# A transformer block on one core: Strassen's scheme on 2x2 blocks for the gates, the convolution inputs and the up projection

## The chip, the core and the metric

The kernel runs on one core of a Trainium2 chip. The metric is the device time of one execution in microseconds (us). A core has five engines that run side by side, each through its own instructions in order: PE (TensorE, the matrix products; its weight loads are listed as PEld), DVE (VectorE), ACT (ScalarE), POOL (GpSimd) and SP (SyncE, which issues nearly all DMAs here). PE writes its products into PSUM, eight banks of 128 partitions x 512 fp32 values; everything else lives in SBUF or, through DMAs, in DRAM.

## The reference

The input is x, 1024 rows of 1024 channels. All numbers are fp32.

```python
h = rms_norm(x, norm1_g)
q, k, v, bg, cg, xc = split(h @ w_in)                 # six times 1024 columns
y_attn = chunked_relpos_attention(q, k, v, ...)       # 16 heads, chunks of 64, 8 chunks back
y_conv = bg * (conv_b + depthwise_causal_conv3(cg * xc, conv_w))
g_attn, g_conv = split(sigmoid(h @ w_gate + b_gate))  # w_gate: 1024 x 2048
merged = g_attn * (y_attn @ w_attn_proj) + g_conv * (y_conv @ w_conv_proj)
x = x + merged @ w_out
h2 = rms_norm(x, norm2_g)
u = square(relu(h2 @ w_up))                           # w_up: 1024 x 4096
x = x + u @ w_down                                    # w_down: 4096 x 1024
```

## The kernel before, in words

Activations lie transposed: channels on the 128 partitions, the 1024 sequence positions along the free dimension, in two halves of 512 (`HC`). A product makes, for one output tile of 128 channels and one half, a sum in one PSUM bank over K in k-tiles of 128. To keep fp32 accuracy, each operand is held as a pair: `split` (L81) makes a high part with an ACT copy and a low part, source minus high part, with a DVE subtraction. A k-tile then costs three matmuls of 128x128 by 128x512 (high by high, low by high, high by low), pinned in the order of the code on PE by `pin` (L69).

The stages, in order of time:
- Attention, pair of heads by pair of heads, with the first `NG = 5` of 16 gate tiles woven into the last pair (L528 to L562). The operand `hT` (normalised rows without the row factor, which `rb` brings in later) stands in SBUF as two tiles of 32 KB a partition.
- The gate tiles 5 to 15 (L568), each 2 halves x 8 k-tiles x 3 = 48 matmuls through `t_stages` (L127); the results, times `rb`, go to DRAM (`gD`).
- The three convolution inputs for each of 8 tiles (L582 to L610), 48 matmuls a product, and the convolution on DVE; its result is split into `yc`, which stays in SBUF.
- The projections `cp` (L628), `ap` (L637) and `out` (L652), 384 matmuls each. Their operands `yc`, `aoT`, `mT`, `h2T` are written into SBUF in split form as their producers come out of PSUM.
- Up and down, woven (L723 to L727): 256 of the 4096 hidden channels are made (`up`, 96 matmuls), and while the next 256 are made, these are used (`down`, 96 matmuls over K = 256) and added to 16 accumulators in SBUF (L719). The mean square of the second norm (two fp32 matmuls by ones, a reciprocal on DVE, L672 to L677) sits in the first up group.

Weights come by DMA into a `raw` tile, are split into a `w` tile of a rotating pool, and are used. Each engine's order is made by a planner that runs when the kernel is built: it takes instructions whose inputs and buffers are ready in the order in which the code has them, so a load or a split moves ahead as far as its buffer allows; matmuls stay in the code's order. A pool opened in the space of closed pools waits for the last reader of every tile in the closed pools that it overlaps (unless it asks for less, which neither kernel does).

Of the kernel before, what the change touches and what calls it, by code (L numbers as in the profile page):

```python
# [40 lines left out]
def block_kernel(ctx, tc, x, xt, wqkv, wcnv, wgate, wcp, wap, wout, wup, wdown,  # L41
# [9 lines left out]
    apool = ctx.enter_context(tc.tile_pool(name="apool", bufs=2))  # L51
    dram = ctx.enter_context(tc.tile_pool(name="dram", bufs=1, space=DRAM))
    psmm = ctx.enter_context(tc.tile_pool(name="psmm", bufs=2, space=PSUM))
# [21 lines left out]
    def matmul(ps, lhsT, rhs, start, stop):  # L75
        pin(nc.tensor.matmul(ps, lhsT, rhs, start=start, stop=stop))  # L76
# [33 lines left out]
    def load_t(src, name):  # L110
        return [load_w(src[u], [4, P], f"{name}_{u}") for u in range(2)]
# [8 lines left out]
    banks = [(psmm, "mm")] * 2  # L120
# [6 lines left out]
    def t_stages(src, mov, evac, name, order=None):  # L127
# [6 lines left out]
        def mm(c, kt):  # L134
            def go():
                if kt == 0:
                    st[c] = bank(f"ps_{name}_{c}")
                w = st["w"][kt // 4]
                for n, (i, j) in enumerate(((0, 0), (1, 0), (0, 1))):
                    matmul(st[c][:], w[:, i, kt % 4, :], mov[c][:, j, kt, :],  # L140
                           kt == 0 and n == 0, kt == ND - 1 and n == 2)
# [5 lines left out]
    def t_layout(*a):  # L147
        load, halves = t_stages(*a)
        load()
        for h in halves:  # L150
            for f in h:
                f()

    def new_act(name):
        return [apool.tile([P, 2, ND, HC], F32R, name=f"{name}{c}", tag="act") for c in range(2)]


    hT = new_act("hT")
# [11 lines left out]
    aoD = [[dram.tile([P, HC], F32, name=f"aoD{p}_{c}") for c in range(2)]  # L170
           for p in range(NH // 2)]
    gD = [dram.tile([P, S], F32, name=f"gD{t}") for t in range(16)]
    mcD = [dram.tile([P, S], F32, name=f"mcD{t}") for t in range(ND)]

# [41 lines left out]
    def qkv_stages(p):  # L216
# [39 lines left out]
        def evac(st, ps):  # L256
            hf, s4 = st // 4, st % 4
            qk = ps[:, 0:256].rearrange("p (a b) -> p a b", a=4)
            sq = a1.tile([P, 4, DH], F32, name=f"sq{p}_{st}", tag="sq")
# [78 lines left out]
    def unit_stages(p, c, m, h):  # L338
# [61 lines left out]
        def pv(g):  # L400
            def go():
# [11 lines left out]
                if g == len(groups) - 1:  # L413
# [6 lines left out]
                    if m % 2 and h:  # L420
                        nc.sync.dma_start(aoD[p][m // 2][:], c.ao[:])
# [97 lines left out]
    def gate_stages(t):  # L519
        def ev(c, ps):  # L520
            g = a1.tile([P, HC], F32, name=f"gp{t}_{c}", tag="sq")
            nc.vector.tensor_tensor(g[:], ps[:], rb[:, c * HC:(c + 1) * HC], op=ALU.mult)
            nc.sync.dma_start(gD[t][:, c * HC:(c + 1) * HC], g[:])
        load, halves = t_stages(wgate[t], hT, ev, f"g{t}")
# [40 lines left out]
    wpool = ctx.enter_context(tc.tile_pool(name="wpool", bufs=2, side="right"))  # L565
    psx = ctx.enter_context(tc.tile_pool(name="psx", bufs=6, space=PSUM))
    banks = [(psx, "x")] * 3 + [(psmm, "mm")] + [(psx, "x")] * 3 + [(psmm, "mm")]
# [215 lines left out]
```

## Time and profile before

| | us |
|---|---|
| median of 3 runs (1910.05 to 1911.23) | 1910.75 |
| the profiled execution | 1911.13 |
| its span, from the first to the last instruction | 1909.3 |
| PE busy with matmuls (9268 of them) | 1882.7 |
| DVE busy | 1058.8 |
| ACT busy | 560.7 |
| POOL busy | 164.0 |

The span leaves 1.8 us of the profiled execution outside. A busy time counts how long an engine had an instruction in work; an engine that is busy all the time is not thereby at its peak. The granted clock of TensorE is a share of 2.4 GHz; its other level is 1.2 GHz (0.5).

### The profile page before, as it was taken

The numbers are of one execution on the slowest core, as the hardware profiler recorded it, in microseconds if no ns is written. First come the engines' busy times: TensorE is split into PE (matmuls) and PEld (weight loads), VectorE is DVE, ScalarE is ACT, GpSimd is POOL, SyncE is SP. The second block draws the span as 40 slices with busy tenths as digits, with TensorE's granted clock in tenths as the row PEclk, the third lists the DMA queues.
The fourth block names the chain that finished last, engine by engine and source line by source line (L and its number), as shares of the span: only waits on it lengthen the run. The fifth ranks groups of instructions, "written<-read, shape, count | busy, mean of one in ns | idle before, by whom it ended". The sixth has DMA issues, their size and how long they took to land.

```text
span 1909.3 us, 24631 instructions
## 1 busy us (share of the span) xinstructions
PE 1882.7 (99%) x9268; PEld 1614.8 (85%) x9268; DVE 1058.8 (55%) x1966; ACT 560.7 (29%) x1117; POOL 164.0 (9%) x467
## 2 busy tenths in 40 slices
PE   6899999999999999999999999999999999999999
PEld 6899999999888888888888888888888888888887
DVE  6677877787642234435433445655555555555555
ACT  5455555555431111111232333211111111111110
POOL 5433233233000000000000000000000000000000
PEclk9999999999999999999999999999999999999999
DMA  6443443443322211111364451111111111111112
GB/s 245 111 109 92 104 110 92 111 110 88 111 86 96 94 56 50 50 45 51 109 215 143 144 156 54 36 53 50 50 45 49 52 45 50 50 45 44 50 51 93
DMA packets 91031, 162.08 MB, mean 85 GB/s; under 512 B 10912, under 2 KB 19104, under 8 KB 90912
## 3 DMA queue, kind: packets, MB, share of 16 engines
q1 hardware_dynamic: 90768, 160.48, 28.7%
q8 instruction: 73, 1.20, 0.3%
q14 instruction: 46, 0.38, 0.1%
q10 hardware_dynamic: 144, 0.03, 0.0%
HBM read 114.33 MB, written 20.97 MB: 71 GB/s over the span
## 4 chain that ended last, share of the span: by engine, by line
PE 95%; POOL 2%; DMA 1%; DVE 1%; ACT 1%; issue 0%; SPq 0%; DVEq 0%; POOLq 0%; ACTq 0%
PE ps_u L76 18%; PE pd L76 18%; PE psq L76 12%; PE ps_g L76 9%; PE ps_x L76 5%; PE ps_cp L76 5%; PE ps_o L76 5%; PE ps_ap L76 5%; PE ps_b L76 5%; PE ps_c L76 5%; PE av L76 3%; PE s L76 3%; PE tp L79 3%; POOL qw L115 0%; PE tq L79 0%
## 5 line engine op out<-in xcount | busy, mean ns | idle before, releaser
L76 PE MATMUL psq<-w_q,hT 128*128 128x384 f32 x1536 | 347.9, 352 | 11.2 <-ACT w_q L83 7.6
L76 PE MATMUL ps_u<-h2T,w_u 128*128 128x512 f32 x1536 | 355.2, 392 | 0.0
L76 PE MATMUL pd<-ut,w_d 128*128 128x512 f32 x1536 | 354.0, 391 | 0.0
L76 PEld LDWEIGHTS ps_u<-h2T,w_u 128*128 128x128 f32 x1536 | 288.5, 188 | 63.9 <-issue 1.0
L76 PEld LDWEIGHTS pd<-ut,w_d 128*128 128x128 f32 x1536 | 288.4, 188 | 63.1
L76 PEld LDWEIGHTS psq<-w_q,hT 128*128 128x128 f32 x1536 | 261.7, 193 | 15.2 <-ACT w_q L83 7.6
L719 DVE TENSOR_TENSOR acc<-pd,acc 128x512 f32<-128x512 f32 x256 | 176.5, 690 | 109.9 <-PE pd L76 107.7
L76 PE MATMUL ps_g<-hT,w_g 128*128 128x512 f32 x768 | 187.9, 395 | 0.0
L76 PEld LDWEIGHTS ps_g<-hT,w_g 128*128 128x128 f32 x768 | 140.6, 188 | 27.2
L689 DVE SCALAR_TENSOR_TENSOR rq<-ps_u,rb 128x512 f32<-128x512 f32 x64 | 44.2, 691 | 135.6 <-PE ps_u L76 135.5
L364 ACT ACTIVATE p<-p,sm 128x640 f32<-128x640 f32 (+4 forms) x128 | 89.7, 701 | 80.9 <-DVE sm L362 80.7
L83 ACT CAST ut<-rq 128x512 fp32r<-128x512 f32 x64 | 39.8, 622 | 216.1 <-DVE rq L691 216.1
L83 ACT CAST w_u<-r_u 128x512 fp32r<-128x512 f32 x64 | 39.9, 624 | 185.3 <-PE pd L76 107.7
L362 DVE CUSTOM_DVE_ANT_0 p<-s,b 128x640 f32<-128x640 f32 (+4 forms) x128 | 83.4, 652 | 12.8 <-PE s L76 9.6
L84 DVE TENSOR_TENSOR pt<-tp,pt 128x512 fp32r<-128x512 f32 (+1 forms) x144 | 84.2, 597 | 11.0 <-ACT pt L83 10.4
L76 PE MATMUL ps_x<-hT,w_x 128*128 128x512 f32 x384 | 89.2, 391 | 0.0
L76 PE MATMUL ps_c<-hT,w_c 128*128 128x512 f32 x384 | 89.2, 391 | 0.0
L76 PE MATMUL ps_b<-hT,w_b 128*128 128x512 f32 x384 | 89.2, 391 | 0.0
L76 PE MATMUL s<-k,q 128*128 128x384 f32 (+3 forms) x384 | 82.0, 322 | 6.4 <-DVE sm L362 6.2
L76 PEld LDWEIGHTS av<-pt,vt 128*128 128x128 f32 x576 | 85.5, 188 | 3.1 <-DVE pt L84 1.2
L83 ACT CAST w_d<-r_d 128x512 fp32r<-128x512 f32 x64 | 39.9, 623 | 164.2 <-PE pd L76 142.9
L76 PE MATMUL ps_cp<-yc,w_cp 128*128 128x512 f32 x384 | 88.1, 391 | 0.0
(116 smaller groups left out, 2232.0 us busy)
## 6 DMA issues: line engine op xcount, KB each, us to landing
q<-qh SPq DMA_DIRECT2D x128, 128.0 KB, 2.3
r_u<-in_wup_dram SPq DMA_DIRECT2D x64, 256.0 KB, 2.6
r_d<-in_wdown_dram SPq DMA_DIRECT2D x64, 256.0 KB, 2.7
r_q<-in_wqkv_dram SPq DMA_DIRECT2D x32, 384.0 KB, 3.5
k<-kh SPq DMA_DIRECT2D x64, 128.0 KB, 2.3
r_g<-in_wgate_dram SPq DMA_DIRECT2D x32, 256.0 KB, 2.7
gD<-gp SPq DMA_DIRECT2D x32, 256.0 KB, 2.0
gl<-gD SPq DMA_DIRECT2D x32, 256.0 KB, 2.9
```

Of the source, the lines that this page charges most:

```text
L76: pin(nc.tensor.matmul(ps, lhsT, rhs, start=start, stop=stop))
L79: pin(nc.tensor.transpose(o, i, ident[:]))
L83: return (nc.scalar.copy(hi, src), nc.vector.tensor_tensor(lo, src, hi.bitcast(F32), op=ALU.subtract))
L84: nc.vector.tensor_tensor(lo, src, hi.bitcast(F32), op=ALU.subtract))
L362: nc.vector.tensor_tensor_reduce(pw, sc[:, k0:k1], biast[p, h][:, 5 * P - w:], -1.0, 3e38, ALU.add, ALU.min, sm[:, 0:1])
L364: nc.scalar.activation(pw, pw, AF.Exp, bias=sm[:, 0:1], scale=-1.0, accum_out=sm[:, 1:2])
L689: nc.vector.scalar_tensor_tensor(q[:], ps[:], 0.0, rb2[:, cc], op0=ALU.max, op1=ALU.mult)
L719: nc.vector.tensor_tensor(a[:], ps[:], a[:], op=ALU.add)
```

## The change

Two neighbouring output tiles (256 channels), both halves of the sequence and two groups of four k-tiles are seen as 2x2 blocks: weights a11, a12, a21, a22 and operand blocks b11 to b22. Strassen's scheme (in Winograd's form) makes the four output blocks from seven block products in place of eight. Each block product sums over 4 k-tiles.

- It applies to 4 gate pairs (tiles 8 to 15), 12 convolution pairs (three inputs for each of 4 pairs of tiles) and 16 up pairs: 32 pairs. Gate tiles 5 to 7 stay plain and run ahead of them.
- The seven weight operands of a pair (`weights`): four loads, four POOL additions or subtractions, seven splits. `w` has 7 buffers, `raw` 5.
- The seven operand blocks (`slot`) are made once a stage, for four "slots" j of two k-tiles each: two source rows from DRAM (512 KB each), four POOL subtractions, seven splits. The `h` operand is made anew from x (`fetch_h`: load and a DVE multiply by gain and row factor); the `h2` operand goes through DRAM (`h2D`). Each slot tile takes 28 KB a partition; two lie on the left side of SBUF, two on the right.
- A narrow `product` runs the seven block products one after another, 12 matmuls each, in three banks: five of them go on adding into bank a, and between two of them ACT or DVE takes the sum so far out. A wide one (the first and the last of each of the two stages) goes through the slots outermost, with seven banks, and combines at the end.
- The other products are `plain`: operands are held per k-tile (8 KB), loaded from DRAM and split (`ktiles`), except for `mk`, which is written as before; the first three output tiles go through the k-tiles outermost with six banks, the last tile too.
- The convolution result (`yD`), the second norm's input (`x2D`, `h2D`) and the hidden activations (`uD`, 32 tiles) go through DRAM. Up runs whole, then down: four passes over K = 1024 each, 64 evictions in place of 256.
- h2 is scaled by `sp` = rb / (1 + rb) before up; the true factor `ms` comes in at the end, after the last pass. `sp` and `ms` take a reciprocal on DVE each.
- One pool of eight PSUM banks serves everything after attention.

The diff, cut to its core:

```diff
+    ps8 = ctx.enter_context(tc.tile_pool(name="ps8", bufs=8, space=PSUM))
+    banks = [(ps8, "x")]
+    jsr = ExitStack()
+    js = [jsr.enter_context(tc.tile_pool(name="jsr", bufs=2, side="right")), None]
...
+    bw = Work("bwa", 5, 2, 3)
+    PROD = {1: ("a11", 0), 2: ("a12", 1), 3: ("s4", 2), 4: ("a22", 6), 5: ("s1", 3),
+            6: ("s2", 4), 7: ("s3", 5)}
+    ORDER = (1, 2, 6, 7, 5, 4, 3)
+    def slot(j, name, fetch):
+        b = []
+        for r in range(2):
+            src = bw.stg(f"b{name}{j}_{r}")
+            fetch(src[:], 2 * j + r)
+            b.append([src[:, cols(c)] for c in range(2)])
+        o = js[j // 2].tile([P, 7, 2, HC], F32R, name=f"o{name}{j}", tag="js")
+        def put(i, x):
+            split(o[:, i, 0, :], o[:, i, 1, :], x)
+        def minus(i, x, y):
+            t = bw.tt(f"t{name}{j}_{i}")
+            nc.gpsimd.tensor_tensor(t[:], x, y, op=ALU.subtract)
+            put(i, t[:])
+            return t[:]
+        put(0, b[0][0])
+        t1 = minus(3, b[0][1], b[0][0])
+        put(1, b[1][0])
+        t2 = minus(4, b[1][1], t1)
+        put(2, b[1][1])
+        minus(5, b[1][1], b[0][1])
+        minus(6, b[1][0], t2)
+        return o
...
+    def weights(src, name):
+        a = {}
+        for n, k in enumerate(("a11", "a12", "a21", "a22")):
+            a[k] = fetch_w(src[n], [4, P], f"{name}_{k}")
+        w = {i: split_w(a[PROD[i][0]], f"{name}_{i}") for i in (1, 2)}
+        for k, x, y, op in (("s1", "a21", "a22", ALU.add), ("s2", "s1", "a11", ALU.subtract),
+                            ("s3", "a11", "a21", ALU.subtract), ("s4", "a12", "s2", ALU.subtract)):
+            if k in ("s1", "s2"):
+                a[k] = wk.tile([P, 4, P], F32, name=f"{name}_{k}", tag="ss", bufs=2)
+            else:
+                a[k] = a[{"s3": "a21", "s4": "a12"}[k]]
+            nc.gpsimd.tensor_tensor(a[k][:], a[x][:], a[y][:], op=op)
+        for i in ORDER[2:]:
+            w[i] = split_w(a[PROD[i][0]], f"{name}_{i}")
+        return w
...
+    def product(src, o, name, ev, wide=False, between=None):
+        w = weights(src, name)
+        if not wide:
+            a = bank(f"pa_{name}")
+            def whole(ps, i, start, stop):
+                for j in range(4):
+                    mms(ps, w, o, i, j, start and j == 0, stop and j == 3, True)
+            whole(a, 1, True, True)
...
+                s1 = snap(a, f"s1_{name}")
+            c = bank(f"pc_{name}")
+            whole(c, 2, True, True)
...
+                ev.put(0, 0, c, s1)
+            whole(a, 6, False, True)
...
+                u2 = snap(a, f"u2_{name}")
+            b = bank(f"pb_{name}")
+            whole(b, 7, True, True)
...
+                s7 = snap(b, f"s7_{name}")
+            whole(a, 5, False, True)
...
+                ev.put(1, 1, a, s7)
+            whole(b, 4, False, True)
...
+                ev.put(1, 0, b, u2)
+            whole(a, 3, False, True)
...
+                ev.put(0, 1, a, None)
+            return
...
+        for j in range(4):
+            for i in ORDER:
+                if j == 0:
+                    ps[i] = bank(f"p{i}_{name}")
+                mms(ps[i], w, o, i, j, j == 0, j == 3, False)
+        s1 = snap(ps[1], f"s1_{name}")
+        u2, u4 = etile(f"u2_{name}"), etile(f"u4_{name}")
+        nc.vector.tensor_tensor(u2[:], ps[6][:], s1[:], op=ALU.add)
...
+            ev.put(0, 0, ps[2], s1)
+        nc.vector.tensor_tensor(u4[:], ps[5][:], u2[:], op=ALU.add)
+        nc.vector.tensor_tensor(u2[:], ps[7][:], u2[:], op=ALU.add)
...
+            v = etile(f"u5_{name}")
+            nc.vector.tensor_tensor(v[:], ps[7][:], u4[:], op=ALU.add)
+        for (r, cc), p, e in (((0, 1), 3, u4), ((1, 0), 4, u2)):
...
+                ev.put(r, cc, ps[p], e)
...
+            ev.put(1, 1, None, v)
...
+        for n, (src, name, ev) in enumerate(jobs):
+            product(src, o, name, ev, n == 0 or free and n == len(jobs) - 1)
+    def fetch_h(d, kt):
+        nc.sync.dma_start(d.rearrange("p (s q) -> p s q", s=NT),
+                          xt[:, :, kt, :].rearrange("s p q -> p s q"))
+        nc.vector.scalar_tensor_tensor(d, d, sv[:, C_G1 + kt:C_G1 + kt + 1], rb[:],
+                                       op0=ALU.mult, op1=ALU.mult)
+    ho = [None] * 4
+    for j in range(2):
+        ho[j] = slot(j, "h", fetch_h)
+    for t in range(NG, 8):
         for f in gate_stages(t):
             f()
-    att.close()
+    aws.close()
+    hpool.close()
+    wk = ctx.enter_context(tc.tile_pool(name="wk", bufs=1))
+    wp = (wk, 7, 5)
+    nw = ctx.enter_context(tc.tile_pool(name="nw", bufs=1))
...
+    jsl = ExitStack()
+    js[1] = jsl.enter_context(tc.tile_pool(name="jsl", bufs=2))
+    for j in range(2, 4):
+        ho[j] = slot(j, "h", fetch_h)
...
+    jobs = [gate_job(4)] + sum([conv_jobs(i) for i in range(4)], [])
+    jobs += [gate_job(i) for i in range(5, 8)]
+    phase(jobs, ho, None, free=True)
+    cvs.close()
+    jsl.close()
+    bw.stack.close()
+    jsr.close()
+    def ktile(pool, name):
+        return pool.tile([P, 2, S], F32R, name=name, tag="kt", bufs=8)
+    def ktiles(pool, name, tiles, first=0):
+        out = []
+        for k in range(ND):
+            src = bw.stg(f"b{name}{k}")
+            nc.sync.dma_start(src[:], tiles[first + k][:])
+            o = ktile(pool, f"{name}{k}")
+            split(o[:, 0, :], o[:, 1, :], src[:])
+            out.append(o)
+        return out
+    def plain(src, o, name, ev, lead=3):
+        def group(ts, outer):
+            w = {t: [load_w(src[t // 2, 2 * (t % 2) + u], [4, P], f"{name}{t}_{u}")
+                     for u in range(2)] for t in ts}
...
+            if outer:
+                for kt in range(ND):
+                    for t in ts:
+                        for c in range(2):
+                            mm(t, c, kt)
...
+        group(list(range(lead)), True)
+        for t in range(lead, ND):
+            group([t], t == ND - 1)
+    kas, kbs = ExitStack(), ExitStack()
+    kta = kas.enter_context(tc.tile_pool(name="kta", bufs=1, side="right"))
+    ktb = kbs.enter_context(tc.tile_pool(name="ktb", bufs=1))
+    bw = Work("bwb", 4, 2, 0, side="left")
...
+    yk = ktiles(kta, "yk", yD)
+    ak = ktiles(ktb, "ak", aoD)
...
+    plain(wap, ak, "ap", ev_ap)
+    nc.vector.tensor_scalar(sp[:], rb[:], 1.0, None, op0=ALU.add)
+    nc.vector.reciprocal(sp[:], sp[:])
+    nc.vector.tensor_tensor(sp[:], sp[:], rb[:], op=ALU.mult)
+    bw.stack.close()
+    kbs.close()
+    jul = ExitStack()
+    js[0] = jul.enter_context(tc.tile_pool(name="jul", bufs=2))
+    bw = Work("bwc", 6, 2, 4, side="left")
...
+    def ev_out(t, c, ps):
...
+        nc.vector.tensor_tensor(a[:], ps[:], a[:], op=ALU.add)
+        nc.sync.dma_start(x2D[t][:, cols(c)], a[:])
+        h = bw.e(f"h{t}_{c}")
+        nc.vector.scalar_tensor_tensor(h[:], a[:], sv[:, C_G2 + t:C_G2 + t + 1],
+                                       sp[:, cols(c)], op0=ALU.mult, op1=ALU.mult)
+        nc.sync.dma_start(h2D[t][:, cols(c)], h[:])
...
+        if c == 1 and t in (1, 3):
+            h2o[t // 2] = slot(t // 2, "n", from_dram(h2D))
+    plain(wout, mk, "o", ev_out)
+    kas.close()
+    jur = ExitStack()
+    js[1] = jur.enter_context(tc.tile_pool(name="jur", bufs=2, side="right"))
+    for j in range(2, 4):
+        h2o[j] = slot(j, "n", from_dram(h2D))
...
+    phase([up_job(i) for i in range(16)], h2o, None, free=True)
+    ms = rb
+    for c in range(2):
+        ps = bank(f"ss2_{c}")
+        matmul(ps[:], ones[:], ssq[:, cols(c)], True, True)
+        m = ms[:, cols(c)]
+        nc.vector.tensor_scalar(m, ps[:], 1.0 / D, EPS, op0=ALU.mult, op1=ALU.add)
+        for _ in range(2):
+            nc.vector.tensor_tensor(m, m, sp[:, cols(c)], op=ALU.mult)
+        nc.vector.reciprocal(m, m)
+    ktd = ctx.enter_context(tc.tile_pool(name="ktd", bufs=1, side="right"))
+    bw = Work("bwd", 4, 2, 0)
...
+    def ktile(pool, name):
+        return pool.tile([P, 2, S], F32R, name=name, tag="kt", bufs=NKD)
+    NKD = 12
+    accp = ctx.enter_context(tc.tile_pool(name="accp", bufs=1))
+    acc = [accp.tile([P, S], F32, name=f"acc{t}") for t in range(ND)]
+    for k in range(4):
+        uk = ktiles(ktd, f"uk{k}_", uD, 8 * k)
+        def ev_d(t, c, ps):
+            a = acc[t][:, cols(c)]
+            if k == 0:
+                nc.scalar.copy(a, ps[:])
+            else:
+                nc.vector.tensor_tensor(a, ps[:], a, op=ALU.add)
+            if k == 3:
+                x2 = bw.e(f"xr{t}_{c}")
+                nc.sync.dma_start(x2[:], x2D[t][:, cols(c)])
+                nc.vector.tensor_tensor(a, a, ms[:, cols(c)], op=ALU.mult)
+                nc.vector.tensor_tensor(a, a, x2[:], op=ALU.add)
+                nc.sync.dma_start(out[t * P:(t + 1) * P, cols(c)], a)
+        plain(wdown[k], uk, f"d{k}_", ev_d)
+    bw.stack.close()
```

## Rows read from the trace of the kernel before

**Rows 1.** The page: busy time by engine; granted TensorE clock in 40 slices.

```profile
PE 1882.7 (99%) x9268; PEld 1614.8 (85%) x9268; DVE 1058.8 (55%) x1966; ACT 560.7 (29%) x1117; POOL 164.0 (9%) x467
...
PEclk9999999999999999999999999999999999999999
```

**Rows 2.** Critical chain, three stages: start us, length us, what.

```profile
673.28 10.99 PE ps_c L76 x48
...
1268.32 21.97 PE ps_u L76 x96
...
1861.60 43.97 PE pd L76 x192
```

**Rows 3.** Up and down: window, length, busy us by engine, clock, DMA.

```profile
1246.40:1861.60 615.20, 615.20 (x2689) 504.76 (x2688) 337.11 (x504) 104.72 (x168) 0.00 (x0) 1.00 0.17 48
```

**Rows 4.** Groups by form: line, engine, operation, xcount | busy us, mean ns.

```profile
L115 POOL TENSOR_TENSOR qw<-qw,nhalf 128x4 f32<-128x4 f32 x64 | 66.3, 1036 | 5.3
...
L84 DVE TENSOR_TENSOR w_u<-r_u,w_u 128x512 fp32r<-128x512 f32 x64 | 44.3, 693 | 13.0 <-ACT w_u L83 11.7
...
L691 DVE TENSOR_TENSOR rq<-ps_u,rq 128x512 f32<-128x512 f32 x64 | 44.0, 688 | 1.1
...
L83 ACT CAST w_u<-r_u 128x512 fp32r<-128x512 f32 x64 | 39.9, 624 | 185.3 <-PE pd L76 107.7 <-PE ps_u L76 64.8 <-PE ps_o L76 10.8
...
L268 POOL TENSOR_TENSOR qw<-qw 128x4 f32<-128x4 f32 x64 | 13.2, 207 | 5.3
...
L661 DVE SCALAR_TENSOR_TENSOR h2T<-acc,sv,h2T 128x512 fp32r<-128x512 f32 x16 | 12.0, 752 | 7.5 <-ACT h2T L660 6.4
...
L84 DVE TENSOR_TENSOR hT<-xt,hT 128x1024 fp32r<-128x1024 f32 x7 | 8.5, 1221 | 2.5 <-ACT hT L83 2.5
...
L203 ACT ACTIVATE xn<-xn 128x1024 f32<-128x1024 f32 x8 | 8.5, 1059 | 0.0
```

**Rows 5.** Line 677: min/median/max ns, first and last start us.

```profile
L677 DVE RECIPROCAL rb<-rb x2: 3353/3354/3354, 1205.0 to 1211.9; 128x512 f32<-128x512 f32 x2
```

**Rows 6.** DMA issues: count, KB each, median us to landing.

```profile
r_g<-in_wgate_dram SPq DMA_DIRECT2D x32, 256.0 KB, 2.7
...
gD<-gp SPq DMA_DIRECT2D x32, 256.0 KB, 2.0
...
acc<-in_xt_dram SPq DMA_DIRECT2D x16, 256.0 KB, 5.2
```

**Rows 7.** Timeline at attention's end: start us, length us, what.

```profile
551.06 9.29 PE L76 MATMUL ps_g<-hT,w_g 128*128 128x512 f32 x40
...
552.68 0.69 DVE L522 TENSOR_TENSOR gp<-ps_g,rb 128x512 f32<-128x512 f32 x1 [0.60 <-PE ps_g L76]
```

**Rows 8.** Timeline at the end of the convolution stage.

```profile
938.38 0.69 DVE L84 TENSOR_TENSOR yc<-y,yc 128x512 fp32r<-128x512 f32 x1
...
939.15 0.80 SPq L618 DMA_DIRECT2D a<-aoD  x2
```

**Rows 9.** Timeline of PE, idle time before it in brackets.

```profile
42.41 0.47 PE L79 MATMUL tq<-ident,qn 128*128 128x128 f32 x1 [4.08 <-DVE qn L279]
...
63.17 0.80 PE L76 MATMUL s<-k,q 128*128 128x256 f32 x2 [5.96 <-DVE sm L362]
```

**Rows 10.** Busy time after those idle stretches, columns as in Rows 3.

```profile
40.00:44.00 4.00, 1.59 (x7) 1.46 (x7) 2.07 (x4) 1.92 (x4) 2.78 (x6) 0.72 0.52 205
44.00:48.00 4.00, 3.38 (x11) 3.00 (x10) 2.41 (x3) 3.63 (x7) 3.59 (x6) 0.50 0.18 40
64.00:68.00 4.00, 4.00 (x14) 4.00 (x14) 1.90 (x8) 0.86 (x3) 0.00 (x0) 0.50 0.02 4
68.00:72.00 4.00, 4.00 (x25) 3.96 (x24) 2.03 (x8) 2.19 (x6) 1.79 (x5) 0.86 0.00 0
```

**Rows 11.** Timeline, last instruction before the final stores.

```profile
1905.59 0.69 DVE L719 TENSOR_TENSOR acc<-pd,acc 128x512 f32<-128x512 f32 x1 [0.69 <-PE pd L76]
```

More of the change, by code (lines that the diff above doesn't have):

```diff
@@ L73, in pin, with matmul @@
         last[0] = ins
[L75 to L76 removed]
+    def matmul(ps, lhsT, rhs, start, stop, chain=False):
+        pin(nc.tensor.matmul(ps, lhsT, rhs, start=start, stop=stop, skip_group_check=chain))
     def transpose(o, i):
@@ L564, in block_kernel @@
     attp.close()
-    wpool = ctx.enter_context(tc.tile_pool(name="wpool", bufs=2, side="right"))
-    psx = ctx.enter_context(tc.tile_pool(name="psx", bufs=6, space=PSUM))
-    banks = [(psx, "x")] * 3 + [(psmm, "mm")] + [(psx, "x")] * 3 + [(psmm, "mm")]
-    for t in range(NG, 16):
-        if t == NG + 2:
-            wp = (wpool, 7, 2)
+    att.close()
+    psm.close()
+    ps8 = ctx.enter_context(tc.tile_pool(name="ps8", bufs=8, space=PSUM))
+    banks = [(ps8, "x")]
+    jsr = ExitStack()
@@ new lines, in from_dram, with cols @@
+    def from_dram(tiles, first=0):
+        return lambda dst, kt: nc.sync.dma_start(dst, tiles[first + kt][:])
+    def cols(c):
+        return slice(c * HC, (c + 1) * HC)
+    def weights(src, name):
[13 more added lines that the diff above has]
+        return w
@@ new lines, in block_kernel, with __init__, total, times @@
+    class Put:
+        sums = False
+        def __init__(self, put):
+            self.put = put
+    class Add:
+        sums = True
+        def __init__(self, add):
+            self.add = add
+    def total(ps, e):
+        if ps is None or e is None:
+            return ps or e
+        nc.vector.tensor_tensor(e[:], ps[:], e[:], op=ALU.add)
+        return e
+    def times(out, ps, e, x):
+        v = total(ps, e)
+        (nc.vector if v is ps else nc.gpsimd).tensor_tensor(out, v[:], x, op=ALU.mult)
@@ new lines, in value, with phase @@
+    def value(out, ps, e):
+        if ps is None or e is None:
+            nc.scalar.copy(out, (ps or e)[:])
+        else:
+            nc.vector.tensor_tensor(out, ps[:], e[:], op=ALU.add)
+    def phase(jobs, o, nxt, free=False):
+        for n, (src, name, ev) in enumerate(jobs):
[5 more added lines that the diff above has]
+                                       op0=ALU.mult, op1=ALU.mult)
@@ L730, in _layout @@
+    bw.stack.close()
 def _layout(inputs):
```

341 lines of the change are left out of this document (181 added, 160 removed).

## The prediction

> **What bounds the kernel now.** I read the page first: PE is busy in 1882.7 of 1909.3 us, at the full clock in every slice [rows 1]. The chain of waits then tells what that busy time consists of: behind attention it is matmuls alone, in stretches that repeat to a hundredth: 48 in 10.99 us, 96 in 21.97, 192 in 43.97 [rows 2], which is 0.2289 us a matmul whatever the stage and however many go to one bank (24 in up, 6 in down). The table by stretch shows no gap behind them: in up and down PE is busy in all of 615.20 us, DVE in 337, ACT in 105, POOL not at all [rows 3]. So behind attention one matmul less is worth 0.2289 us, and work on other engines is free until PE has to wait for it. The time after is therefore the matmuls that go, less the waits that the new stage borders bring.
>
> **What goes.** An ordinary pair of tiles takes 2 x 2 x 8 x 3 = 96 matmuls, a Strassen pair 7 x 4 x 3 = 84. 32 pairs save 384 matmuls: 384 x 0.2289 = 87.9 us. PE's count should fall from 9268 to 8884. Attention, the first eight gate tiles, cp, ap, out and down keep theirs.
>
> **Inside a Strassen stage: costed at nothing.** A pair now gives PE 84 x 0.2289 = 19.2 us. DVE in a narrow up pair: 7 splits and 7 combining or squaring instructions at 0.69 us = 9.7 us; ACT: 7 casts and 4 copies at 0.62 = 6.8 us; SP: 4 loads and 4 stores. POOL has 4 additions of 128x512, which the trace does not show. From below they cost the 0.21 us of its 4-column addition, from above that instruction's dearest form (1.04 us) plus DVE's whole time for this shape (0.69): 1.73. I take 0.21 + 0.69 = 0.9, 3.6 us a pair [rows 4]; at 1.73 it would be 6.9, still under 19.2. The weights of the next pair come one by one as the seven buffers fall free, each some 16 us ahead of its use. In bank a, PE goes on adding only after ACT or DVE has read the sum so far, and between the two stand 12 matmuls on another bank, 2.75 us, against a copy of 0.62 or an addition of 0.69. If that cover is gone, it is the rival on the slow side below. The lead and tail groups of the plain products also have their cover: a k-tile of the lead group is 18 matmuls, 4.1 us, against 1.22 us of DVE for its split. Down's 64 evictions in place of 256 take about 130 us off DVE (192 x 0.69), off the path: nothing.
>
> **The borders.** T is the end of the last matmul of the old stage. What decides is that a new pool waits for all readers of the pools in whose space it lies. The trace has such a case: the loads into a new pool (L618) start 0.08 us after the split that last reads the closed one (938.38 + 0.69, then 939.15) [rows 8]. I let ready instructions go in the order of the code.
>
> - *Attention to gate tile 5.* The eight-bank pool takes the banks in which gate tile 4 is evicted. Now PE runs on (40 matmuls without a gap) while that eviction goes from 552.68 to 553.37; afterwards PE waits from about 552.5: +0.9 us [rows 7]; between 0 and 1.5.
> - *Gates to Strassen (A).* The weight pool lies where hT lay, so the first load starts at T: lands at T + 2.7 [rows 6], cast 0.62, subtraction 0.69: first matmul at T + 4.1. DVE then has 14 splits to make, 7 weights and the 7 operands of slot 2, whose pool also waits for the old stage: 14 x 0.69 = 9.7 us from T + 3.4, the last at T + 13.1. PE needs all seven weights in the first slot's 21 matmuls (4.8 us unhindered), so that ends at T + 13.8, not T + 4.8: +9.0. Slot 3 needs two more loads (x comes in short pieces, 5.2 us for 256 KB [rows 6]) and 7 splits behind slot 2's, and is ready by about T + 20; PE comes to it at T + 23.5. Least: 4.1 (weights first, all else covered). Most: 14, if slot 3 is 5 us late.
> - *Strassen to cp (B).* The k-tiles on the right are 64 KB, the slots there were 56 KB, so their pool also overlaps the work tiles and waits until the last gate block is stored. After the wide product DVE has three combinations left when PE stops: done at T + 2.3, store 2.0 [rows 6], then ACT 1.06 and DVE 1.22 for the first k-tile [rows 4]: PE goes on at T + 7.0: +7.0. Between 0 (no such wait) and 8.
> - *cp to ap to out.* ak is loaded under cp; mk's last tile is needed 29 us into out. Nothing; against it at most the 2.8 us of that tile's eviction and split.
> - *Out to up (E).* Six weights are split before T; the seventh waits for T, and behind the last two evictions (2.9 us with the 0.75 us form) and slot 2's 7 splits (4.8 us), which the code has earlier, it is ready at T + 8.4, where PE wants it at T + 4.1: +4.3. Slot 3 (store 2.0, load some 4, splits 5 us) is ready at about T + 15, wanted at T + 19. Between 0 and 9.
> - *Up to down (F).* PE first does the two fp32 products for the mean square (2.0 us). DVE combines and squares until T + 4.9 (11 instructions of 0.69, begun at T - 2.7). Then come, in the order of the code, the two mean-square chains: 3 x 0.69 and a reciprocal of 3.35 us [rows 5], 5.4 each, 10.8 in all, though nothing needs them before the fourth pass. Only behind them come the first k-tiles (pool free at T) and five of six weights: 15.7 + 2 x 1.22 + 4 x 0.69 = T + 21, where PE would have been at that weight at T + 5: 16 late. If the planner puts what is ready at T ahead of the chains, the k-tiles from the third on wait behind them: 13; if the chains come last, some 5. I take 13; bounds 5 and 17.
> - *The end (G).* Three DVE instructions for each half in place of one: last of six at T + 3.6, where it was T + 0.7 [rows 11]: +2.9; between 1.4 and 4.
>
> **The clock.** After an idle stretch of 4.08 us and one of 5.96 us [rows 9] the granted clock went to 0.50. The loss is PE's busy time by the missing share: 1.59 x 0.28 + 3.38 x 0.50 = 2.1 us, and 4.00 x 0.50 + 4.00 x 0.14 = 2.6 us [rows 10]. I take 2.5 us for each of A, B, E and F: 10.0.
>
> **Sum.** 0.9 + 9.0 + 7.0 + 4.3 + 13.0 + 2.9 + 10.0 = 47.1 us back of 87.9: 40.8 us gained. The profiled execution's 1911.1 becomes 1870.3; the median of the runs stands 0.4 us under it: 1870. With every term at its lower end (0 + 4.1 + 0 + 0 + 5 + 1.4, two falls of the clock) 15.5 come back: 1838. At the upper end (1.5 + 14 + 8 + 2.8 + 9 + 17 + 4 + 10) 66: 1889.
>
> **A rule weighed.** In this trace POOL works only on a few columns at a time (0.21 us) and DVE's split, with both inputs in SBUF, takes 0.69 us in stages without POOL work [rows 3, 4]; nothing shows them side by side. The Trainium skill, "SBUF — State Buffer", section "Who interferes with whom", says that a DVE instruction with two SBUF inputs and a GpSimd instruction that reads SBUF exclude each other for the whole instruction. No run here shows it yet. Taken as a mechanism of this kernel, in which each POOL addition holds up a split for its own 0.9 us, a pair has 9.7 + 3.6 = 13.3 us of DVE under 19.2 of PE: still nothing inside the stages. At A four weight additions fall among the 14 splits: +3.6, and at E perhaps as much: about 1876. That is the third rival.
>
> **The rivals.**
> - *The borders are mostly hidden.* The planner has the first operands ready at each border, and A, B, E and F cost together what they do at their lower ends. For it: DVE and ACT are idle half the time and more [rows 1], and the wide products free their slots one after another. Against it: the pool waits above, which no idle engine shortens. 15 us back: 1838.
> - *Slower: the sums taken out of bank a hold PE.* In each of the 28 narrow products there are four places where PE adds on to a bank that another engine must first have read. If the reader stands behind other work (splits of the next pair, the convolution's instructions over 1024 columns at over 1 us each [rows 4], a store that holds a work tile), PE waits there beyond its 2.75 us. 28 x 4 = 112 places; the 40.8 us are gone at 0.36 us a place. One 0.69 us split too many at each: +77, 1947. For it: DVE and ACT serve in order, and 14 DVE instructions a pair come close together. Against it: 2.75 us is four of them, and half of DVE's time is free.
> - *POOL holds DVE up*, as above: 1876.
> - That the change doesn't do what it says is only this: that a matmul in the new order takes longer than 0.2289 us. Before it depends neither on the stage nor on the number to a bank [rows 2]; I give it nothing of its own.
>
> **How the numbers follow.** Forecast 0.58 (1855 to 1890); hidden borders 0.22 (1830 to 1855); POOL 0.08 (inside the forecast's range); slower inside the products 0.12, spread from 1885 to 1950. The range that holds 8 in 10 leaves out the lowest half of the hidden case and most of the slow one: 1838 to 1898. A difference under 0.2% (4 us: 1907 to 1914.5) can't be told from none here. Faster: the first three cases and a small part of the slow one, 0.89; the same 0.03; slower 0.08.
>
> **What would show it.** Right: 8884 matmuls; 19.2 us from one Strassen pair to the next, 21.97 us for two plain tiles; PE idle stretches at four borders of 9, 7, 4 and 13 us, each followed by a stretch at clock 0.5; at up to down DVE in two reciprocals of 3.35 us while PE waits for a split of uk or w; the last DVE instruction 3.6 us behind the last matmul. Wrong: waits of PE inside Strassen pairs on a copy or an addition (the slow rival); DVE splits of over 1 us beside POOL additions (the third); borders without idle time (the first), or a wait of PE on a DMA, which I have nowhere but in A.

## The result: slower by 1.8%

| | before | changed |
|---|---|---|
| median of the runs | 1910.4 us (4 runs) | 1942.53 us (4 runs) |
| profiled execution, its span | 1911.1, 1909.3 | 1948.01, 1946.2 |
| mean granted clock | 0.996 | 0.971 |

The ratio is 1.0175, 95% interval [1.0156, 1.0193]: 32 us more, where 40 us less were forecast. The count of matmuls is as predicted. The profiled execution is the slowest of the four; the other three lie within 0.7 us of each other. The page after, against [rows 1]:

```profile
PE 1832.3 (94%) x8884; PEld 1551.2 (80%) x8884; DVE 1070.5 (55%) x1870; ACT 698.2 (36%) x1337; POOL 472.1 (24%) x661
PE   7899999999994999999799999499999979999998
PEclk9999999999997999999899999699999989999999
```

PE has 384 matmuls less and is busy only 50.4 us less; it idles for 113.9 us of the span where it idled for 26.6. The clock, full in every slice before, dips in four places, and PE has holes in the same ones. These are the borders. The table by stretch (time, PE, PEld, DVE, ACT, POOL busy with counts, granted clock, DMA share, GB/s), against [rows 3, 10]:

```profile
587.00:637.00 50.00, 24.27 (x87) 18.48 (x87) 36.02 (x33) 15.98 (x28) 19.90 (x14) 0.73 0.26 79
637.00:889.80 252.80, 252.80 (x1093) 204.70 (x1092) 140.01 (x163) 86.45 (x142) 124.40 (x80) 1.00 0.26 80
928.70:945.00 16.30, 2.02 (x4) 1.23 (x5) 7.59 (x12) 4.36 (x5) 0.00 (x0) 0.61 0.81 274
1213.20:1277.20 64.00, 33.77 (x109) 23.98 (x108) 45.13 (x53) 20.78 (x37) 32.24 (x21) 0.71 0.46 154
1277.20:1544.00 266.80, 266.80 (x1153) 216.04 (x1152) 137.54 (x195) 86.31 (x151) 85.57 (x56) 1.00 0.34 109
1563.70:1585.00 21.30, 8.14 (x20) 5.12 (x19) 21.20 (x24) 4.37 (x5) 0.00 (x0) 0.68 0.64 218
```

Rows two and five lie inside the Strassen stages: PE is busy throughout, 13 pairs of 84 matmuls in 252.80 us, 19.45 each (19.2 forecast). The other rows are borders: gates to Strassen (A) idles for 25.7 us, Strassen to cp (B) for 14.3, out to up (E) for 30.2, up to down (F) for 13.2. What PE waited for (total, times, longest):

```profile
PE p_u L74 <- DVE x L951: 26.2, 6, 8.3
PE p_g L74 <- DVE w_g L82: 22.0, 2, 13.4
PE ps_cp L74 <- DMA byk<-yD: 14.4, 1, 14.4
PE ps_d L74 <- ACT uk L81: 9.9, 1, 9.9
PE p_g L74 <- issue: 3.7, 1, 3.7
PE ps_d L74 <- DVE uk L82: 3.3, 1, 3.3
```

**E, the largest.** PE waits six times for the eviction of an *out* product. Between two waits it does three matmuls, at first in 0.85 and 0.94 us, then in 1.62 each time: the granted clock is 0.50 from 1220 to 1248 us. PE's timeline (start, us, work, idle before and its releaser):

```profile
1213.06 0.85 PE L74 MATMUL p_u<-on,w_u 128*128 128x512 f32 x3
1216.28 0.94 PE L74 MATMUL p_u<-on,w_u 128*128 128x512 f32 x3 [2.37 <-DVE x L951]
...
1237.63 1.62 PE L74 MATMUL p_u<-on,w_u 128*128 128x512 f32 x3 [4.56 <-DVE x L951]
1247.52 2.90 PE L74 MATMUL p_u<-on,w_u 128*128 128x512 f32 x6 [8.27 <-DVE x L951]
```

DVE in turn stood for x to land. From 1150 to 1256 us:

```profile
DVE x L951 <- DMA x<-in_xt_dram: 23.5, 10, 4.6
```

Each x takes 3.0 to 4.9 us from issue to landing, and is issued late: x (L948) and the h of the same eviction (L953) come from one tag of six tiles, given out in the code's order, so that the loads can't run ahead past the h tiles of earlier evictions. One load stands ahead of the evictions; the next is issued at 1154.80, behind the first eviction, and then one comes behind each.

```profile
1127.28 0.38 SPq L949 DMA_DIRECT2D x<-in_xt_dram  x1
```

So sixteen evictions dragged on from 1153 to 1252 us, while *out's* matmuls were done at 1213; the first wide product of up needs the banks that they free.

**A.** DVE's timeline behind the last gate eviction, with two of POOL's additions:

```profile
587.65 0.68 DVE L936 TENSOR_SCALAR sp<-rb 128x1024 f32<-128x1024 f32 x1
588.36 6.55 DVE L937 RECIPROCAL sp<-sp 128x1024 f32<-128x1024 f32 x1
595.80 1.74 DVE L82 TENSOR_TENSOR oh<-th,oh 128x512 fp32r<-128x512 f32 x1
...
598.63 1.72 POOL L615 TENSOR_TENSOR th<-bh,th 128x512 f32<-128x512 f32 x1
...
603.82 2.36 DVE L82 TENSOR_TENSOR w_g<-r_g_a,w_g 128x512 fp32r<-128x512 f32 x2
...
617.60 1.28 DVE L82 TENSOR_TENSOR w_g<-r_g_a,w_g 128x512 fp32r<-128x512 f32 x2
...
622.97 1.29 POOL L644 TENSOR_TENSOR c_s<-c_s,r_c_a 128x512 f32<-128x512 f32 x1
```

First comes a reciprocal that belongs behind ap (L937) and that the planner took forward; then splits of 1.74 us where [rows 4] have 0.69, in turn with POOL's additions, which mostly take 1.70 to 1.72 us there and 1.30 alone. The weights' splits stand behind them.

### The profile page after: what moved, and what is told of

It reads as the page before. It is cut to its first block, busy times and chain, and to the rows that moved or that the text cites. A ratio compares the mean times of both kernels' runs of the same rounds, so it can differ in the third digit from the quotient of the medians.

```text
span 1946.2 us, 24851 instructions
## 1 busy us (share of the span) xinstructions
PE 1832.3 (94%) x8884; PEld 1551.2 (80%) x8884; DVE 1070.5 (55%) x1870; ACT 698.2 (36%) x1337; POOL 472.1 (24%) x661
## 3 DMA queue, kind: packets, MB, share of 16 engines
q8 instruction: 70, 1.15, 0.2%
## 4 chain that ended last, share of the span: by engine, by line
PE 60%; DMA 4%; DVE 3%; issue 1%; POOL 0%; ACT 0%; SPq 0%; DVEq 0%; POOLq 0%; ACTq 0%
PE ps_d L74 18%; PE pa_u L74 8%; PE ps_cp L74 5%; PE ps_ap L74 4%; PE pb_u L74 4%; PE pa_b L74 2%; PE pa_x L74 2%; PE pa_c L74 2%; PE pc_u L74 2%; PE p_g L74 2%; PE ps_o L74 1%; PE pa_g L74 1%; PE pb_b L74 1%; PE pb_x L74 1%; PE pb_c L74 1%; DMA x<-in_xt_dram 1%
## 5 line engine op out<-in xcount | busy, mean ns | idle before, releaser
L74 PE MATMUL ps_d<-uk,w_d 128*128 128x512 f32 x1536 | 361.5, 396 | 13.2 <-ACT uk L81 9.9
L74 PEld LDWEIGHTS ps_d<-uk,w_d 128*128 128x128 f32 x1536 | 289.1, 188 | 85.9 <-issue 10.7
L74 PE MATMUL pa_u<-on,w_u 128*128 128x512 f32 x672 | 162.6, 393 | 0.0
L74 PEld LDWEIGHTS pa_u<-on,w_u 128*128 128x128 f32 x672 | 126.1, 188 | 29.7
L74 PE MATMUL ps_cp<-yk,w_cp 128*128 128x512 f32 x384 | 92.9, 403 | 14.4 <-DMA byk<-yD 14.4
L74 PE MATMUL ps_g<-hT,w_g 128*128 128x512 f32 x384 | 100.2, 399 | 1.4 <-DVE gp L521 1.4
L74 PEld LDWEIGHTS ps_cp<-yk,w_cp 128*128 128x128 f32 x384 | 73.7, 193 | 33.6 <-issue 14.7
L74 PE MATMUL ps_o<-mk,w_o 128*128 128x512 f32 x384 | 90.0, 395 | 0.4 <-DVE x L951 0.4
L74 PE MATMUL av<-pt,vt 128*128 128x256 f32 (+1 forms) x576 | 86.7, 273 | 1.0 <-DVE pt L82 1.0
L74 PE MATMUL ps_ap<-ak,w_ap 128*128 128x512 f32 x384 | 87.2, 389 | 0.0
```

What stands on the lines that cost most here:

```text
L74: pin(nc.tensor.matmul(ps, lhsT, rhs, start=start, stop=stop, skip_group_check=chain))
```

## The experiments

Times are medians; the changed kernel has 1942.5, and 0.2% (4 us) is about the interval of one comparison.

**sp held back.** `gate` keeps an instruction, in the planner's order, behind the matmul that stands last before it in the code. The same edit at L936 and L938:

```
-    nc.vector.reciprocal(sp[:], sp[:])
+    gate(nc.vector.reciprocal(sp[:], sp[:]))
```

> The three instructions that make 1/(1+rb)*rb for the second norm (L936 to L938) are held behind ap's last product; nothing else is edited. Theory: at the border from the gate tiles to the Strassen products DVE has these first (0.68 + 6.55 us and a multiplication) while PE waits for a split of w_g, so the 25.7 us in which PE idles at 587 to 637 us fall by 7 to 9, and with the clock that comes back earlier the time falls by 8 to 11 us from 1942.5. Rival: the splits are held by their own rate beside the POOL additions and by the loads, so the reciprocal only fills time in which DVE would wait anyway: the idle time stays above 22 us and the time falls by under 4.

1938.7 us (ratio 1.0147 [1.0132, 1.0162]): 4 less, under the theory's 8 to 11. The wait for DVE's split of w_g fell from 22.0 to 14.0, but 3.4 us of waiting for ACT's cast of it came in, and border A still idled for 20.9 us (585 to 635 us, since the gates ended 1.3 us earlier in this execution):

```profile
585.00:635.00 50.00, 29.12 (x105) 21.24 (x105) 32.27 (x35) 17.77 (x31) 21.12 (x15) 0.73 0.31 100
```

The reciprocal holds the border, and the next thing stands right behind it. So neither theory holds in full: the idle time fell by 4.8 us, for 7 to 9, and the time by the rival's under 4.

**The sums on DVE.**

```
-            nc.gpsimd.tensor_tensor(t[:], x, y, op=ALU.subtract)
+            nc.vector.tensor_tensor(t[:], x, y, op=ALU.subtract)
...
-            nc.gpsimd.tensor_tensor(a[k][:], a[x][:], a[y][:], op=op)
+            nc.vector.tensor_tensor(a[k][:], a[x][:], a[y][:], op=op)
```

> The Strassen sums of weights and of operands (4 a pair and 4 a slot, L615 and L644) go from POOL to DVE; nothing else is edited. Theory: a POOL addition and a DVE split shut each other out, so without POOL the splits of w_g and oh take 0.69 us instead of 1.7 at the gates' border; its last w_g split comes some 6 to 9 us earlier although DVE has 8 sums more there, and the time falls by 6 to 12 us. Rival: the splits are long for another reason (loads landing in SBUF, ACT's casts): they stay at 1.7 us, DVE's added sums (4 x 0.69 us a pair, 12 a border) lengthen the borders, and the time rises by 3 to 10 us. Inside the stages neither expects a wait: 18 DVE instructions of 0.69 us = 12.4 us under 19.4 us of matmuls.

1935.1 us (1.0128 [1.0113, 1.0143]): 7.5 less although DVE has more to do, inside the theory's 6 to 12. The operands' splits at border A, 587 to 637 us, of the changed kernel (busy, mean ns):

```profile
L82 DVE TENSOR_TENSOR oh<-th,oh 128x512 fp32r<-128x512 f32 x8 | 9.6, 1215 | 0.0
L82 DVE TENSOR_TENSOR oh<-bh,oh 128x512 fp32r<-128x512 f32 x6 | 7.6, 1274 | 0.0
```

and with the sums on DVE:

```profile
L82 DVE TENSOR_TENSOR oh<-th,oh 128x512 fp32r<-128x512 f32 x8 | 5.4, 684 | 0.0
L82 DVE TENSOR_TENSOR oh<-bh,oh 128x512 fp32r<-128x512 f32 x6 | 4.0, 675 | 0.0
```

ACT's casts beside them took the same (616 ns), and the share of the DMA engines was 0.28 for 0.26, so the long splits were POOL's doing; the third rival's mechanism is shown. The Trainium skill, "SBUF — State Buffer", section "Who interferes with whom", says that a DVE instruction with two SBUF inputs contends with a GpSimd instruction that reads SBUF, and calls the port pair that they share an exclusive lock. The trace agrees in kind: 0.69 and 1.30 us apart, 1.74 and 1.7 side by side. But a split and an addition together start every 1.67 us (the `on` splits shown under the next run), less than the 1.99 us of the two alone, so that the lock does not cover the whole of both.

The place was not the expected one. At A PE idles for 23.5 us, 2.2 less; the larger part came off at E, where the waits for L951 had 26.2 us, and 24 to 26 in the other runs that leave E alone:

```profile
587.00:637.00 50.00, 26.50 (x97) 19.63 (x96) 36.75 (x48) 16.53 (x29) 0.11 (x1) 0.73 0.28 87
```

```profile
PE p_u L74 <- DVE x L951: 18.5, 5, 5.4
```

**h tiles of their own.**

```
-        h = bw.e(f"h{t}_{c}")
+        h = bw.tt(f"h{t}_{c}")
```

> In out's eviction the second result (h, L953) is taken from the four half tiles that the slots' sums use instead of from the six tiles of x (L948); nothing else is edited, no memory is added. Theory: x of an eviction could not be loaded before the previous eviction had its h tile, so that out's evictions ran one after another, each behind a load of 3 to 5 us; with tiles of their own the loads run ahead, the evictions keep up with the matmuls, the six waits of p_u for DVE L951 (26.2 us together) go, and PE's idle time between 1213 and 1277 us falls from 30 to 4 to 9; with the half clock in that stretch gone the time falls by 28 to 38 us. Rival: the evictions are slow because the x rows come in 512-byte pieces and POOL's 16 squares and the slots' sums hold DVE: the six waits stay in other places and the time falls by under 10 us.

1925.3 us (1.0082 [1.0067, 1.0097]): 17 less from one word, between the theory's 28 to 38 and the rival's under 10. Six loads now run ahead, where one did:

```profile
1125.68 3.13 SPq L949 DMA_DIRECT2D x<-in_xt_dram  x6
```

The six waits for L951 are gone, DVE no longer waits for x. What is late next, on DVE:

```profile
1225.34 1.74 DVE L82 TENSOR_TENSOR on<-tn,on 128x512 fp32r<-128x512 f32 x1
1227.01 1.74 DVE L82 TENSOR_TENSOR on<-bn,on 128x512 fp32r<-128x512 f32 x1
1228.67 1.75 DVE L82 TENSOR_TENSOR w_u<-r_u_a,w_u 128x512 fp32r<-128x512 f32 x1
```

and PE behind it:

```profile
1230.47 18.07 PE L74 MATMUL p_u<-on,w_u 128*128 128x512 f32 x65 [12.37 <-DVE w_u L82]
```

That is the seventh weight behind slot 2's splits, which the prediction had at E for 4.3 us; beside POOL's additions it is 12.4. With the sums on DVE as well (run c1 below) it is 4.5:

```profile
PE p_u L74 <- DVE w_u L82: 4.5, 1, 4.5
```

So the hold by the h tiles is shown, and so is the one behind it, whose 12.4 us stand in the place of the rest of the expected gain.

**The mean square later.** L989 to L996 go into down's loop:

```
     for k in range(4):
         uk = ktiles(ktd, f"uk{k}_", uD, 8 * k)
+        if k == 1:
+            for c in range(2):
+                ps = bank(f"ss2_{c}")
...
```

> The mean square of the second norm (two fp32 products, two chains of three DVE instructions and a reciprocal of 3.3 us, L989 to L996) goes from ahead of down's first quarter to behind it; nothing else is edited. Theory: DVE then makes the first k-tiles' splits as soon as they have landed, the wait of ps_d for the DVE split of uk (3.3 us) goes, the one for ACT (9.9 us: the load is issued only when uD is stored) stays: idle time at this border 13.2 to 10, the time falls by 3 to 6 us. Rival: the two fp32 products no longer cover part of the wait for the load, so that this wait grows by the 2 to 4 us that they took: no change within 2 us.

1944.0 us (1.0178 [1.0161, 1.0195]): no change, the rival's time. F's wait is now one, put down to a weight's load, and as long as the two before (9.9 + 3.3):

```profile
PE ps_d L74 <- DMA r_d<-in_wdown_dram: 13.6, 1, 13.6
```

The first k-tile is no earlier, though: ACT's cast of it waits 10.12 us for its load and starts 1.15 us before PE goes on.

**Waits by tile, and a queue of their own.** The first on every pool behind attention; then, on top, the second:

```
-    kta = kas.enter_context(tc.tile_pool(name="kta", bufs=1, side="right"))
+    kta = kas.enter_context(tc.tile_pool(name="kta", bufs=1, side="right", reuse_waits="tile"))
...
-            nc.sync.dma_start(src[:], tiles[first + k][:])
+            nc.gpsimd.dma_start(src[:], tiles[first + k][:])
```

> The pools opened behind attention wait for the old tiles under each single tile and no longer for the whole closed pool; the code and its order are not edited. Theory: at Strassen to cp the first k-tile's load waits for the last gate's store only because a pool does, so with tile-wise waits it is issued some 5 to 7 us earlier and the wait of ps_cp falls from 14.4 to 7 to 9 us; at up to down the same takes 3 to 5 us off the 9.9; the time falls by 8 to 14 us from 1942.5. Rival: SP's queue has the last stores ahead of the loads in its order and waits there for DVE's last combinations whatever the pools wait for: both waits stay within 2 us, and so does the time.

> As the run with tile-wise waits (1943.6 us), and the loads of the k-tiles' sources (byk, of ao, buk) are issued from POOL's queue and not from SP's. Theory: what holds them at Strassen to cp and at up to down is SP's order, in which they stand behind the last stores; from a queue of their own they start before these, the wait of ps_cp falls from 12.9 to 3 to 7 us, that of ps_d from 10.7 to 4 to 8, and the time by 8 to 16 us, to 1928 to 1936. Rival: the staging tiles lie over tiles that the last product still uses, so the loads start no earlier: 1940 to 1946.

1943.6 and 1944.4 us: no change, both theories fell. In the first run the loads of the first two yk were still issued at 933.66, behind others in SP's queue; in the second they were issued 30 us before they were wanted (POOL), so its rival's mechanism fell too, and ACT still cast them late:

```profile
898.13 1.35 POOL L864 DMA_DIRECT2D byk<-yD  x2
```

```profile
939.57 0.72 ACT L907 ACTIVATE gl<-gl,sv 128x512 f32<-128x512 f32 x1 [6.64 <-DMA gl<-gD]
940.19 1.98 ACT L81 CAST yk<-byk 128x1024 fp32r<-128x1024 f32 x2
```

ACT stood in a gate's sigmoid, whose load comes late, ahead of the cast. So the sigmoid was put behind its product, on top of the run just shown, and alone:

```
-        nc.scalar.activation(g[:], g[:], AF.Sigmoid, bias=sv[:, C_BG + t:C_BG + t + 1])
+        gate(nc.scalar.activation(g[:], g[:], AF.Sigmoid, bias=sv[:, C_BG + t:C_BG + t + 1]))
```

> The run with tile-wise waits and the k-tiles' loads on POOL's queue (1944.4 us), with the sigmoids held behind their products. Theory as in the run before it: ps_cp's wait from 12.7 to 2 to 5 us, 1934 to 1938. Rival: unchanged, 1941 to 1947.

> The changed kernel with the sigmoids held behind their products and nothing else. Theory (two holds one behind the other, each enough by itself): the first load of yk is still issued at 935.6 behind the last stores, so the wait of ps_cp stays at 11 to 14.4 us and the time at 1939 to 1945. Rival (the sigmoid alone made the wait, the load's place in SP's queue was harmless): it falls by 5 us or more, and the time to 1934 to 1938.

1938.6 and 1942.5 us. With early loads the wait at B fell from 12.7 to 8.1 us (the theory had 2 to 5); alone the edit does nothing (12.4 us), as its theory had it. What is left of the wait in the first:

```profile
934.37 1.99 ACT L81 CAST yk<-byk 128x1024 fp32r<-128x1024 f32 x2 [4.14 <-DMA gD<-u_g]
```

That is the last gate block's store: yk lies where its work tile lay. B has three holds, one behind the other, and the prediction had only this last one (7.0 us).

**Where the operands lie.** Between the kernels the step from matmul to matmul differs, to which the prediction gave nothing. Chains of waits (start, us, count) of the changed kernel; the stages of [rows 2] have 228.9 ns throughout:

```profile
1035.91 87.06 PE ps_ap L74 x384
1122.97 26.61 PE ps_o L74 x114
1579.66 359.57 PE ps_d L74 x1531
```

ap's moving operand is on the left of SBUF: 87.06 / 384 = 226.7 ns. out's and down's are on the right: 26.61 / 114 = 233.4 ns. Weights are on the left for all. The kernel before has moving operands on the left and weights on the right from its eighth gate tile on. Tested by moving down's operands to the left, and in the kernel before the weights:

```
-    ktd = ctx.enter_context(tc.tile_pool(name="ktd", bufs=1, side="right"))
+    ktd = ctx.enter_context(tc.tile_pool(name="ktd", bufs=1))
```

```
     att.close()
+    wps.close()
+    wpool = ctx.enter_context(tc.tile_pool(name="wpl", bufs=2))
+    wp = (wpool, 7, 2)
```

> Down's operand tiles uk go from the right end of SBUF to the left one, where the weights are; nothing else is edited. Theory: the step from one matmul to the next depends on where the moving operand lies against the weights: 226.7 ns for ak (left), 233.3 for yk, mk and uk (right); then down's 1536 matmuls take 6.6 ns less each, 10.1 us, and the time falls by 9 to 11 us from 1942.5. Rival: the step belongs to the stage (what DMA and the other engines do beside it): it stays at 233 and the time within 3 us.

> The kernel before, with its weight tiles on the left of SBUF from the convolution on, where its moving operands are (they were on the right); nothing else is edited. Theory: the step between matmuls falls from 228.9 to 226.7 ns as with ak and uk: 5376 matmuls x 2.2 ns = 11.8 us, less 2 to 5 us for the new pool at the gates' end: 1900 to 1905. Rival: weights do not matter, only the moving operand's place: 1910 to 1915.

1930.5 us (1.0107 [1.0092, 1.0123]), 12 less: the theory, and a little. Down's chain there:

```profile
1576.12 349.36 PE ps_d L74 x1531
```

It is 10.2 us shorter over the same 1531 matmuls, 6.7 ns each (both chains begin at half clock, so their means stand above the step).

The kernel before with its weights moved: 1909.4 us (0.9993 [0.9983, 1.0002]). The step did fall: 48 matmuls start every 10.88 us, 226.7 ns, where [rows 2] have 10.99.

```profile
704.41 11.04 PE L76 MATMUL ps_b<-hT,w_b 128*128 128x512 f32 x48
715.29 11.04 PE L76 MATMUL ps_c<-hT,w_c 128*128 128x512 f32 x48
```

But the time missed the theory, since the new pool cost a new wait:

```profile
PE ps_c L76 <- ACT w_c L83: 7.8, 1, 7.8
```

with a low clock behind it. So both operands' places count, and most of the saved 11.8 us was spent on a border.

The Strassen products have half of their slots on either side, whose steps have a mean of 230.0 ns. A wide product, which goes from one side to the other once, comes close to it; a narrow one, which changes sides every six matmuls, does not (up's last wide product, then one of a narrow product's seven):

```profile
1544.25 19.34 PE p_u L74 x84
```

```profile
636.83 2.78 PE pa_c L74 x12
```

19.34 / 84 = 230.2 ns, 2.78 / 12 = 231.7. By these rows the change of sides costs some 20 ns each twelve matmuls; no run tests it by itself.

**Together.** sp late, sums on DVE and h tiles (c1); with uk on the left and waits by tile (c2); with POOL's queue and the mean square later (c3); with the first product's weights ahead of slots 2 and 3 in the code (c4); with the sigmoids held (d1). c4's edit:

```
+    first["g4"] = weights(wgate[4], "g4")
     for j in range(2, 4):
         ho[j] = slot(j, "h", fetch_h)
...
-        w = weights(src, name)
+        w = first.pop(name, None) or weights(src, name)
```

> The edits of three earlier runs in one: sp behind ap's last product, the Strassen sums on DVE, h tiles of their own in out's eviction. Alone they gave 4, 7 and 17 us. Theory (three causes, each in its own place): the sum, 29 us, and 5 to 8 us more, since the wait for the w_u split that the third edit left (12.4 us behind `on` splits of 1.7 us beside POOL's) shortens when these take 0.69: 1904 to 1910. Rival (the first two take the same wait of p_g at the gates' border, and the freed time is taken up by DVE's further sums): 1914 to 1920.

> As the run before it, with uk on the left and tile-wise waits of the pools as well. Theory: 10 us from the step of down's matmuls and 8 to 14 from the earlier loads at two borders on top of it: 1882 to 1892, below the kernel before. Rival: neither counts, 1904 to 1910.

> The best so far (1898.7 us: sp late, sums on DVE, h tiles of their own, uk on the left, tile-wise waits) with the k-tiles' loads on POOL's queue and the mean square behind down's first quarter. Theory: both border waits (13.0 us of ps_cp, 13.2 of ps_d) fall by half or more, 1880 to 1889. Rival: the loads are held by memory, or the first k-tile's wait turns into one for the weights' load r_d, as where the mean square alone was moved: 1895 to 1901.

> As c3, with the seven weights of the first Strassen product made ahead of slots 2 and 3 in the code. Theory: at the gates' border PE waits 17.5 us for w_g because the 14 operand splits stand ahead on ACT and DVE; with the weights first the first slot's 21 matmuls start some 10 us earlier, and slots 2 and 3 are then late by less: idle 17.5 to 8 to 12, time 5 to 10 us under c3. Rival: the work of DVE at this border (33 instructions of 0.69 us = 23 us against 19 us of matmuls) only changes its order; PE waits for the splits of slot 2 and 3 instead: within 3 us of c3.

> The fastest so far (c4, 1881.1 us) with the gates' sigmoids (L907) held behind the product that they scale. Theory: at Strassen to cp the first k-tiles have landed long before, but ACT sits in a sigmoid of a gate tile whose load comes late, ahead of the cast of yk; behind the product it holds nothing, the wait of ps_cp falls from 12.8 to 2 to 5 us and the time to 1869 to 1875. Rival: the k-tile's own place in SBUF is what comes late: the wait stays above 10 us and the time within 3 us.

| | us | ratio to before, 95% |
|---|---|---|
| c1 | 1909.8 | 0.9994 [0.9985, 1.0004] |
| c2 | 1898.7 | 0.9936 [0.9922, 0.9951] |
| c3 | 1891.9 | 0.9901 [0.9886, 0.9916] |
| c4 | 1881.1 | 0.9846 [0.9831, 0.9860] |
| d1 | 1878.2 | 0.9822 [0.9804, 0.9841] |

Three small edits give back the whole loss (c1: 33 us, 29 by their sum). c2 misses its theory (1882 to 1892): its 11 us are the operands' place, as far as the runs above tell (waits by tile alone gave nothing). c3 lies between its theory and its rival. c4 has 10.8 us, a little over its theory: PE waited at A for weights behind 14 splits of operands that it needs only later, and its waits for p_g there fell from 18.7 to 7.4 us. d1 misses its theory (1869 to 1875): its gain over c4 is inside the intervals, and its wait at B fell from 12.8 to 8.4. It is 1.8% faster than the kernel before, 8 us above the forecast of 1870, with the same 8884 matmuls. Its waits behind attention that are over 4 us:

```profile
PE ps_cp L74 <- ACT yk L81: 8.4, 1, 8.4
PE ps_d L74 <- ACT uk L81: 7.5, 1, 7.5
PE p_u L74 <- DVE w_u L82: 6.5, 1, 6.5
PE p_g L74 <- ACT w_g L81: 4.8, 2, 4.1
```

## Why the prediction was wrong

The mechanism of the saving was right, and so was its size: 384 matmuls, and no wait of PE inside a Strassen pair, so that the slow rival (sums taken out of bank a) fell. The miss is 77.7 us between the profiled executions, 1870.3 against 1948.0 (72.5 between forecast and median). It lies in three terms: idle time, the clock and the step.

- *Idle time at the borders: 37.1 us forecast, 87.3 measured (113.9 - 26.6).* The step that failed most is "cp to ap to out: nothing", with E's +4.3 built on it: E cost 30.2, and giving h its own tiles took 17 us off the time. The prediction counted matmuls and DVE time for out and did not ask for its evictions how far their loads can run ahead; six tiles for two names answer that. A cost 25.7 for 9.0: the reciprocal brought forward (PE's idle time at A fell by 4.8 us in its run), POOL's additions (2.2) and weights behind operands in the code (11.3 from c3 to c4). What is left, 7.4 in c4, is near the 9.0. The prediction let ready instructions go in the order of the code and did not search the later code for what would be ready early. Of POOL it had the rule, at 0.08, and an addition at 0.9 us; the row now is 1.30, inside its bounds. At A the rule costs about what the third rival gave it (2.2 for 3.6), at E more: 12.4 for 4.5 at the seventh weight. B cost 14.4 for 7.0: the predicted hold is there (8.1 when alone), with SP's order and a sigmoid ahead of it.
- *F: 13 forecast, 13.2 measured, by another way.* The forecast had the mean-square chains hold the splits; they make 3.3 us of it, and the k-tile's load, issued at 1570.7 when uD's stores had landed, 9.9. Taking the chains away changed nothing: a right size of a wrong reason.
- *The clock: 10.0 forecast, about 18.* PE's busy time by the missing share, in rows of 1 us each, is 4.3 us at A, 3.2 at B (where 0.50 lasts until 949), 7.8 at E and 2.9 at F. (The border rows above would give 24.27 x 0.27 + 2.02 x 0.39 + 33.77 x 0.29 + 8.14 x 0.32 = 19.7, but their means take in the clock of idle time.) The forecast took 2.5 us a border from two single gaps; that fits B and F. Where short work and gaps alternate, as in A and E, the clock stayed at 0.50 longer, at E from 1220 to 1248 us.
- *The step between matmuls: nothing forecast, about 16 us.* 1536 x 4.4 ns in down, 768 x 4.4 in cp and out, 384 x -2.2 in ap, 2688 x 2.6 in Strassen (252.80 us / 1092 = 231.5 ns): 6.8 + 3.4 - 0.8 + 7.0. It was read as a constant because the stages of [rows 2] all have their operands on the same sides.

50.2 + 8.2 + 16.4 = 74.8 of the 77.7 us; the last 3 have no place. The end (G) came near the forecast: the last DVE instruction ends 3.1 us behind the last matmul, for 3.6. What stays open: why the place of the two operands moves the step, and F's remaining wait, whose load waits for work tiles of the last up product (that wait was read in the trace, not taken away).

## What to carry to other kernels

Here the saving inside the stages came almost as counted, and the borders decided. In a kernel bound by one engine, then, for each border list what every engine's queue holds in the planner's order, long instructions from later code too, and ask of each load which tile must be free before it can be issued. Taking one hold away shows the next one behind it, so price a border by the whole row of holds and try the edits together. Check the place of the operands in SBUF before the step of a matmul is taken over from another layout.

## What the hardware showed that was not expected

- The step of fp32r matmuls of 512 columns was 226.7 ns in stages with moving operand and weights both on the left of SBUF, 228.9 with the weights on the right, 233.3 with the moving operand on the right; moving down's operands gave 12 us. Narrow Strassen products, whose moving operand changes sides every six matmuls, had 231.7.
- A POOL addition of 128x512 took 1.30 us alone and mostly 1.70 to 1.72 beside DVE's splits, which took 1.74 there and 0.69 alone; one of each started every 1.67 us.
